# Two queues for one stream of weights: which engine issues the loads of the conditioning slots

## The chip, the cores and the metric

The kernel runs on one core of one Trainium2 chip. The metric is the device time in microseconds (us) of one execution, as the median of several runs. The engines are TensorE (PE in the profile, with its weight loads as PEld), VectorE (DVE), ScalarE (ACT), GpSimd (POOL) and SyncE (SP). SP does no arithmetic here: it issues the DMAs.

## The reference, cut to what matters

Two decoder layers over 256 tokens of width 2048, in float32. Each layer has a mixer (layer 0: sliding-window attention and a pooling mixer; layer 1: an mLSTM and block attention), then a gated feed-forward part with a short convolution. Every part is wrapped in RMSNorm and in a conditioning that is computed from one vector `c`:

```
c_act = silu(c)
mod = c_act @ ada_w[layer] + ada_b[layer]          # 2048 -> 6 x 2048
sh_m, sc_m, gt_m, sh_f, sc_f, gt_f = split(mod, 6)
h = rms_norm(x, norm_mix_pre) * (1 + sc_m) + sh_m
x = x + gt_m * rms_norm(mixer(h), norm_mix_post)
h = rms_norm(x, norm_ffn_pre) * (1 + sc_f) + sh_f
x = x + gt_f * rms_norm(conv_ffn(h), norm_ffn_post)
```

The twelve sections of `mod` need 2 x 2048 x 12288 weights, each used once, for a product of one vector with a matrix. All other weights are used for products with 256 tokens.

## The kernel before, in words

All weights stream from HBM once, in tiles of 1 MB (128 partitions x 2048 floats). Two kinds of tile share the pool `wst`, told apart by a tag:

- Tag "w", three slots: the weights of the products with 256 tokens ("split weights"). `load_split` (line 306) loads a tile and splits each half of it into a high and a low part, the high one by ACT (line 303), the low one by DVE (line 304), so that TensorE can multiply in three terms (`mm3`, lines 339 to 341) or two (`Halves.add`, lines 358 and 361). Six buffers hold high halves and five hold low halves.
- Tag "a", two slots (`SLOTS = (3, 2)`, line 25): the weights of the conditioning. They come in four streams. `ada_first` (line 523) multiplies 8 tiles on TensorE (line 532), `ada_gate` (line 541) another 16 (line 547), and `ada_rows` (line 558) handles the other 168: one DVE instruction multiplies a tile by the vector `c_row` and sums along it (line 564), and a short add of the bias follows (line 565). Of the 8 tiles of `ada_first` and of the 24 of `ada_m`, which `ada_rows` takes first, every other one goes into a "w" slot instead (`ATAG = "aw"`, line 27). So 4 + 12 + 16 + 144 = 176 loads go through the two "a" slots.

The conditioning is worked off behind the rest: `Behind.push` (line 257) emits the next tile's load and its arithmetic, and `Behind.step` (line 266), called once for each `load_split`, pushes at a pace that the kernel sets for each stage (up to 2 tiles for each tile of split weights in layer 0's mixer, between 0.2 and 1 in the feed-forward part). `need` pushes what is due before a norm.

Every load, of either tag, is issued by line 299 from SP, and SP issues in order. So a load of one kind that waits for its slot holds back those of the other kind behind it. A slot of tag "w" comes free when DVE has made the low part of the second half (line 304); a slot of tag "a" when line 564 has read it (or TensorE at line 547). POOL has 48 short instructions: constants at the start, masks (lines 238 to 242), and memsets of attention, pooling and gate tiles (lines 748, 860, 945, 969, 971). Each engine's order, POOL's and SP's among them, is laid down when the program is built.

In time the stages are: to about 38 us the start (x, the vector c, `ada_first`); to about 165 us layer 0's combined input projection (`first_of_all`) beside `ada_m`; to about 345 us attention, pooling and the output projection of layer 0 beside `ada_gate` and the first of the DVE rows; then layer 0's feed-forward part, layer 1's mixer from about 1100 us and its feed-forward part from about 1470 us. The DVE rows end near 1610 us.

Of the kernel before, what the change touches and what calls it, by code (L numbers as in the profile page):

```python
# [178 lines left out]
def trunk(ctx: ExitStack, tc: tile.TileContext, A, out):  # L179
    nc = tc.nc  # L180
# [115 lines left out]

    def load(src, shape=(128, NK, 128), tag="w"):
        w = wst.tile(list(shape), F32, name="w", tag=tag, bufs=SLOTS[tag == "a"])
        nc.sync.dma_start(w, src)
        return w  # L300

    def split(src, hi, lo):
# [3 lines left out]
    def load_split(src, shape=(128, NK, 128), later=False):  # L306

        w = load(src, shape)
        n = shape[1]
        parts = []  # L310

        def half(i):
            a, b = (n // 2) * i, n if i else n // 2
            hi = whp.tile([128, b - a, shape[2]], F32R, name="whi", tag="whi")
            lo = wlp.tile([128, b - a, shape[2]], F32R, name="wlo", tag="wlo")
            with ExitStack() as queue:
                if behind.splits > 0:
                    behind.splits -= 1
                    for ins in behind.marks:
                        queue.enter_context(tc.issue_after(ins))  # L320
                split(w[:, a:b, :], hi, lo)
            parts.append((hi, lo))
        half(0)
        if not later:
            half(1)
        behind.step()

        def at(i, m=1):
            if i < 0:
                return half(1)  # L330
            i, j = divmod(i, n // 2)
            if m == 1:
                return tuple(p[:, j, :] for p in parts[i])
            return tuple(p[:, j:j + m, :].rearrange("p a b -> p (a b)") for p in parts[i])
        return at
# [187 lines left out]
    def ada_first():  # L523

        for i, s in enumerate((SC_M, SH_M)):
            ps = bank((128, 4, 32))
            for k4 in range(4):
                w = load(A["ada_pe"][i, k4], (128, 4, 512), ATAG[k4 % 2])
                for r in range(4):
                    k = 4 * k4 + r  # L530
                    for j in range(4):
                        nc.tensor.matmul(ps[32 * j:32 * j + 32], c_rep[:, k, :], w[:, r, 128 * j:128 * j + 128],
                                         start=k == 0, stop=k == NK - 1, tile_position=(0, 32 * j))
                if k4 < 3:
                    yield
            tr = sml.tile([128, 4, 32], F32, name="tr", tag="t", bufs=4)
            nc.vector.transpose(tr.rearrange("p a b -> p (a b)"), ps.rearrange("p a b -> p (a b)"))
            nc.vector.tensor_tensor(mod[0, s][:, 0:4], tr[:, :, 0], ada_b(0, s)[:, 0:4], op=OP.add)
            yield

    def ada_gate():

        ps = bank((128, 512))
        for k in range(NK):
            w = load(A["ada_g"][k], (128, 1, D), "a")
            for j in range(4):
                nc.tensor.matmul(ps[32 * j:32 * j + 32, :], c_rep[:, k, :], w[:, 0, 512 * j:512 * j + 512],  # L547
                                 start=k == 0, stop=k == NK - 1, tile_position=(0, 32 * j))
            if k < NK - 1:
                yield  # L550
        for i in range(2):
            c = slice(8 * i, 8 * i + 8)
            tr = sml.tile([128, 8, 32], F32, name="tr", tag="t", bufs=4)
            nc.vector.transpose(tr.rearrange("p a b -> p (a b)"), ps[:, 256 * i:256 * i + 256])
            nc.vector.tensor_tensor(mod[0, GT_M][:, c], tr[:, :, 0], ada_b(0, GT_M)[:, c], op=OP.add)
        yield
# [646 lines left out]
```

## Time and profile before

| What | Value |
|---|---|
| median of 3 runs (lowest to highest) | 2221.96 us (2221.46 to 2225.73) |
| the profiled execution's own time | 2221.93 us |
| its span, first to last instruction | 2220.2 us |
| mean granted TensorE clock | 0.979 of full |
| busy: PE, DVE, ACT, POOL | 97%, 76%, 52%, 0% |
| moved by DMA | 578.42 MB, 261 GB/s on average |

The profiled execution lies 0.03 us below the median, and its time is 1.7 us longer than its span. A busy PE is not PE at its peak, since ends of matmuls are modelled; the granted clock of a stretch says at which of its two levels TensorE ran.

### The profile page before, as it was taken

The page shows a single profiled execution, that of the slowest core. Times are in us where ns is not written, and L with a number is a line of the kernel's source. Part 1 is how long each engine was busy: PE and PEld are TensorE (multiplying, and loading weights), DVE is VectorE, ACT ScalarE, POOL GpSimd, SP SyncE. Part 2 cuts the span into 40 slices and gives each one's busy share as a digit, 9 for nine tenths or more (in the row PEclk, how much of TensorE's full clock was granted, in tenths as well). Part 3 has the DMA queues.
Part 4 walks back from the last instruction along what each step waited for, and adds up shares of the span by engine and source line. Part 5 has one row for each costly group of instructions (what it writes and reads, how often), then busy time and mean ns, then how long its engine had stood idle before and what let it go on. Part 6 is the DMA issues. An engine that isn't in the chain of part 4 may idle for free.

```text
span 2220.2 us, 31418 instructions
## 1 busy us (share of the span) xinstructions
PE 2143.8 (97%) x12390; PEld 1857.7 (84%) x12390; DVE 1686.2 (76%) x2533; ACT 1153.6 (52%) x1790; POOL 10.4 (0%) x48
## 2 busy tenths in 40 slices
PE   7888998999999999999899999989999999999998
PEld 5886677997888888888797898878888888888886
DVE  4896798898899899887799867579955665665566
ACT  3345655464555455445576655555545544554453
POOL 1000000000000000000000000000000000000000
PEclk8899998999999999999999999989999999999999
DMA  9987886889889888887387635558855555555553
GB/s 372 348 334 280 322 339 258 328 310 350 308 325 341 331 322 332 330 332 263 135 300 275 229 132 190 190 189 307 319 209 184 188 197 189 190 188 194 188 190 114
DMA packets 81373, 578.42 MB, mean 261 GB/s; under 512 B 9156, under 2 KB 9156, under 8 KB 11464
## 3 DMA queue, kind: packets, MB, share of 16 engines
q1 hardware_dynamic: 81224, 576.40, 70.5%
q8 instruction: 97, 1.59, 0.3%
q14 instruction: 52, 0.43, 0.1%
HBM read 574.27 MB, written 2.10 MB: 260 GB/s over the span
## 4 chain that ended last, share of the span: by engine, by line
PE 90%; DVE 6%; ACT 2%; DMA 1%; issue 1%; SPq 0%; DVEq 0%; ACTq 0%
PE ps L358 28%; PE ps L361 15%; PE ps L340 14%; PE ps L339 14%; PE ps L341 14%; DVE w L564 2%; DVE wlo L304 2%; ACT g L582 1%; PE ps L758 1%; PE ps L547 1%; ACT whi L303 0%; PE ps L795 0%; PE ps L805 0%; DVE x L696 0%; DMA x<-in_x_dram 0%
## 5 line engine op out<-in xcount | busy, mean ns | idle before, releaser
L304 DVE TENSOR_TENSOR wlo<-w,whi 128x1024 fp32r<-128x1024 f32 (+1 forms) x706 | 847.7, 1218 | 314.9 <-PE ps L340 155.6
L303 ACT ACTIVATE whi<-w 128x1024 fp32r<-128x1024 f32 (+1 forms) x706 | 737.4, 1055 | 587.0 <-PE ps L341 281.4
L358 PE MATMUL ps<-g,whi 128*128 128x512 f32 x2736 | 654.4, 391 | 0.0
L358 PEld LDWEIGHTS ps<-g,whi 128*128 128x128 f32 x2736 | 501.9, 188 | 100.5 <-issue 1.2
L340 PE MATMUL ps<-wlo,g 128*128 128x512 f32 (+1 forms) x1152 | 429.1, 373 | 2.2 <-DVE wlo L304 2.2
L339 PE MATMUL ps<-whi,g 128*128 128x512 f32 (+1 forms) x1152 | 428.8, 373 | 0.3 <-ACT g L303 0.2
L341 PE MATMUL ps<-whi,g 128*128 128x512 f32 (+1 forms) x1152 | 428.2, 372 | 0.6 <-DVE g L304 0.6
L564 DVE SCALAR_TENSOR_TENSOR w<-w,c_row 128x2048 f32<-128x2048 f32 x168 | 383.7, 2285 | 3.9 <-DMA w<-in_ada_dve_dram 3.8
L361 PEld LDWEIGHTS ps<-g,wlo 128*128 128x128 f32 x2736 | 350.5, 191 | 13.6
L361 PE MATMUL ps<-g,wlo 128*128 128x256 f32 x2736 | 354.9, 283 | 0.0
L340 PEld LDWEIGHTS ps<-wlo,g 128*128 128x128 f32 x1152 | 217.1, 188 | 42.9 <-DVE wlo L304 4.0
L339 PEld LDWEIGHTS ps<-whi,g 128*128 128x128 f32 x1152 | 216.9, 188 | 40.5 <-issue 1.9
L341 PEld LDWEIGHTS ps<-whi,g 128*128 128x128 f32 x1152 | 216.9, 188 | 38.7 <-DVE g L304 1.5
L339 PE MATMUL ps<-g,whi 128*128 128x256 f32 x800 | 234.9, 297 | 13.7 <-ACT whi L303 7.1
L340 PE MATMUL ps<-g,whi 128*128 128x256 f32 x800 | 235.0, 295 | 0.3 <-DVE g L630 0.3
L341 PE MATMUL ps<-g,wlo 128*128 128x256 f32 x800 | 231.3, 294 | 1.4 <-DVE wlo L304 1.3
L339 PEld LDWEIGHTS ps<-g,whi 128*128 128x128 f32 x800 | 161.2, 203 | 17.3 <-ACT whi L303 8.7
L340 PEld LDWEIGHTS ps<-g,whi 128*128 128x128 f32 x800 | 161.8, 202 | 2.4 <-DVE g L630 2.3
L341 PEld LDWEIGHTS ps<-g,wlo 128*128 128x128 f32 x800 | 160.4, 202 | 2.4 <-DVE wlo L304 2.0
L366 ACT ACTIVATE low<-ps 128x256 f32<-128x256 f32 x156 | 59.5, 381 | 94.8 <-PE ps L361 94.4
L1133 DVE SCALAR_TENSOR_TENSOR z<-low,smalls,z 128x255 f32<-128x255 f32 (+1 forms) x148 | 71.3, 482 | 25.1 <-ACT z L1131 23.5
L1131 ACT ACTIVATE z<-low,smalls 128x256 f32<-128x256 f32 x74 | 44.6, 602 | 84.5 <-DVE low L367 84.5
(195 smaller groups left out, 1173.8 us busy)
## 6 DMA issues: line engine op xcount, KB each, us to landing
w<-in_up_dram SPq DMA_DIRECT2D x148, 1024.0 KB, 4.8
w<-in_ada_dve_dram SPq DMA_DIRECT2D x144, 1024.0 KB, 6.9
w<-in_down_dram SPq DMA_DIRECT2D x88, 1024.0 KB, 4.8
w<-in_up_first_dram SPq DMA_DIRECT2D x28, 1024.0 KB, 7.7
w<-in_ada_m_dram SPq DMA_DIRECT2D x24, 1024.0 KB, 7.5
w<-in_ev_first_dram SPq DMA_DIRECT2D x20, 1024.0 KB, 7.1
w<-in_ada_g_dram SPq DMA_DIRECT2D x16, 1024.0 KB, 4.8
w<-in_ev_out_dram SPq DMA_DIRECT2D x16, 1024.0 KB, 7.8
```

The lines of the kernel that those rows point to most:

```text
L303: nc.scalar.activation(hi, src, AF.Copy)
L304: nc.vector.tensor_tensor(lo, src, hi.bitcast(F32), op=OP.subtract)
L339: nc.tensor.matmul(ps, lh, rh, start=first, stop=False, **kw)
L340: nc.tensor.matmul(ps, lh, rl, start=False, stop=False, **kw)
L341: nc.tensor.matmul(ps, ll, rh, start=False, stop=last, **kw)
L358: nc.tensor.matmul(self.ps.rearrange("p a b -> p (a b)"), w(k)[0], act(k).both, start=k == 0, stop=False, skip_group_check=True)
L361: nc.tensor.matmul(self.ps[:, 0, :], w(k)[1], act(k)[0], start=False, stop=k == NK - 1, skip_group_check=True)
L366: nc.scalar.activation(low, self.ps[:, 1, :], AF.Copy)
L547: nc.tensor.matmul(ps[32 * j:32 * j + 32, :], c_rep[:, k, :], w[:, 0, 512 * j:512 * j + 512], start=k == 0, stop=k == NK - 1, tile_positio ...
L564: nc.vector.scalar_tensor_tensor(w, w, 1.0, c_row, op0=OP.mult, op1=OP.mult, accum_out=m)
L1131: nc.scalar.activation(z, pg, AF.Identity, scale=cw(2, f), bias=sm(f"ffn_b{l}", f))
L1133: nc.vector.scalar_tensor_tensor(z[:, lag:], pg[:, :T - lag], cw(2 - lag, f), z[:, lag:], op0=OP.mult, op1=OP.add)
```

## The change

The issuing engine of a load is now chosen by its tag: loads into the two "a" slots are issued from GpSimd's queue, all others from SyncE's as before. Slots, order of the calls, sizes and arithmetic are the same.

```
     def load(src, shape=(128, NK, 128), tag="w"):
         w = wst.tile(list(shape), F32, name="w", tag=tag, bufs=SLOTS[tag == "a"])
-        nc.sync.dma_start(w, src)
+        (nc.gpsimd if tag == "a" else nc.sync).dma_start(w, src)
         return w
```

## Rows read from the trace of the kernel before

**Rows 1.** The page: busy times by engine, and the chain that ended last.

```profile
PE 2143.8 (97%) x12390; PEld 1857.7 (84%) x12390; DVE 1686.2 (76%) x2533; ACT 1153.6 (52%) x1790; POOL 10.4 (0%) x48
...
PE 90%; DVE 6%; ACT 2%; DMA 1%; issue 1%; SPq 0%; DVEq 0%; ACTq 0%
```

**Rows 2.** Stretches: us, PE PEld DVE ACT POOL busy, PE clock, DMA share, GB/s.

```profile
38.00:165.00 127.00, 114.19 (x815) 110.17 (x816) 112.83 (x150) 49.03 (x61) 0.00 (x0) 0.89 0.91 346
165.00:250.00 85.00, 78.89 (x495) 52.84 (x496) 51.17 (x151) 45.74 (x113) 0.67 (x6) 0.96 0.78 283
250.00:345.00 95.00, 87.03 (x408) 67.72 (x404) 88.94 (x160) 55.85 (x127) 1.90 (x4) 0.99 0.87 336
...
500.00:1050.00 550.00, 548.91 (x2890) 472.50 (x2889) 476.52 (x633) 279.32 (x369) 0.00 (x0) 1.00 0.86 324
```

**Rows 3.** Waits of SP's queue, whole span: us in total, times, longest.

```profile
SPq L299 <- DVE wlo L304: 1426.0, 305, 11.0
SPq L299 <- DVE mod L565: 157.0, 38, 9.9
SPq L299 <- DVE w L564: 133.2, 42, 6.7
...
SPq L299 <- PE ps L547: 36.5, 15, 5.9
```

**Rows 4.** Timelines of SP and PE at the start: start us, us, instruction.

```profile
1.24 1.37 SPq L299 DMA_DIRECT2D w<-in_ada_pe_dram  x3
...
17.91 7.19 PE L896 MATMUL ps<-g,ones 1*128 1x512 f32 x8 [4.85 <-DMA g<-in_c_row_dram]
```

**Rows 5.** Waits of PE (40 to 165 us) and DVE (80 to 160 us); one stretch, columns of rows 2.

```profile
PE ps L339 <- ACT whi L303: 3.4, 5, 1.6
...
DVE g L434 <- PE ps L341: 5.6, 6, 1.1
...
101.30:104.70 3.40, 3.40 (x18) 3.40 (x18) 2.64 (x3) 2.00 (x2) 0.00 (x0) 0.50 0.99 398
```

**Rows 6.** Timelines of SP and PE, and PE's waits, 186 to 250 us.

```profile
189.61 17.43 SPq L299 DMA_DIRECT2D w<-in_ada_g_dram  x6
...
194.43 1.94 PE L547 MATMUL ps<-w,c_rep 128*32 128x512 f32 x8 [0.55 <-DMA w<-in_ada_g_dram]
...
205.59 1.06 PE L547 MATMUL ps<-w,c_rep 128*32 128x512 f32 x8 [0.87 <-DMA w<-in_ada_g_dram]
...
PE ps L878 <- DVE pdiff L871: 4.7, 4, 2.2
```

**Rows 7.** Timeline of POOL: start us, us, instruction [idle before, releaser].

```profile
3.86 0.42 POOL L248 TENSOR_SCALAR_AFFINE_SELECT after<-after 128x256 f32<-128x256 f32 x1
...
278.62 1.06 POOL L239 TENSOR_SCALAR_AFFINE_SELECT dist<-dist 128x256 f32<-128x256 f32 x1
...
1127.17 0.52 POOL L969 MEMSET g<- 128x512 f32 x1 [18.42 <-PE ps L624]
```

**Rows 8.** Timelines of SP and DVE, landing of in_ada_dve, PE's waits; 250 to 345 us.

```profile
254.02 4.34 SPq L299 DMA_DIRECT2D w<-in_ada_dve_dram  x2
...
251.70 2.29 DVE L564 SCALAR_TENSOR_TENSOR w<-w,c_row 128x2048 f32<-128x2048 f32 x1
...
261.13 2.29 DVE L564 SCALAR_TENSOR_TENSOR w<-w,c_row 128x2048 f32<-128x2048 f32 x1
...
309.18 2.29 DVE L564 SCALAR_TENSOR_TENSOR w<-w,c_row 128x2048 f32<-128x2048 f32 x1 [0.36 <-DMA w<-in_ada_dve_dram]
...
DMA to landing us min/median/max: 4.7/6.3/6.4
...
PE ps L340 <- DVE wlo L304: 2.0, 3, 1.2
```

**Rows 9.** Timeline of DVE: two instructions on 256 elements.

```profile
35.49 0.29 DVE L629 CAST g<-h 128x256 fp32r<-128x256 f32 x1 [0.69 <-ACT h L627]
35.82 0.42 DVE L630 TENSOR_TENSOR g<-h,g 128x256 fp32r<-128x256 f32 x1
```

More of the change, by code (lines that the diff above doesn't have):

```diff
@@ L298, in load @@
         w = wst.tile(list(shape), F32, name="w", tag=tag, bufs=SLOTS[tag == "a"])
-        nc.sync.dma_start(w, src)
+        (nc.gpsimd if tag == "a" else nc.sync).dma_start(w, src)
         return w
```

## The prediction

> **What bounds the kernel now.** I read the page first. TensorE is busy for 97% of the span and the chain that ended last lies on it for 90%, on DVE for 6% and on DMA for 1% [rows 1]. So the loads as such are hardly on the path: a change of queues can win or lose only where TensorE waits, or where DVE or ACT, which feed it, wait. The table by stretch says where that can be. From 500 to 1050 us TensorE is busy for 548.91 of 550 us at full clock, though 0.86 of the DMA time is taken: nothing can be won there, and a late conditioning load is covered by TensorE's own work. The three earlier stretches are different: 38 to 165 us (DVE busy for 112.83 of 127, DMA 0.91, clock 0.89), 165 to 250 us, and 250 to 345 us (DVE 88.94 of 95) [rows 2]. There three engines and the DMAs run close together, and any one may give or take a few microseconds.
>
> The waits of SP's own queue show what the change is about. SP stands 1426.0 us waiting for the split of a weight tile, which is the normal state of a queue that prefetches into three slots. But it also stands 157.0 + 133.2 + 36.5 = 326.7 us because an "a" slot is still being read by lines 564/565 or 547 [rows 3]. For that time a load of split weights behind it could not start. Now the two are separated.
>
> **The change part by part.** The profiled execution took 2221.93 us, span 2220.2, and the sum is made against that; it is 0.03 us below the median of the runs shown. A measurement of this kernel can tell about 0.2%, or 4.4 us, from no change.
>
> 176 issues leave SP's queue, and 176 arrive in POOL's. No byte, slot or instruction on another engine is added or removed. SP's saved issue time (1.37 us for three, under 0.5 us each [rows 4]) is worth nothing by itself: SP waits far longer than it issues.
>
> **What POOL needs for an issue** is not in this trace. From below it costs nothing over SP. From above it costs POOL's costliest instruction, 1.06 us [rows 7], plus a whole 2.29 us DVE instruction [rows 8] if the two hinder each other: 3.35 us. I take 1.06 us, since an instruction of POOL is the nearest row, and call it the delay. By the Trainium skill (DMA: Bandwidth & Descriptors, section "Latency and other measured facts") the first byte comes about 0.4 us later on the GpSimd path than on the SP path; with that for the delay, terms 3 and 4 below would shrink to about 0.7 us together and the sum to about +0.7 us. No row here shows it.
>
> *Term 1, the start.* SP issues the first three tiles of `ada_first` at 1.24 us [rows 4]. Two of them move to POOL, which stands in its constants until 4.28 us (3.86 + 0.42) [rows 7]. TensorE waits 4.85 us at 17.91 for the pieces of `c_row`, which lie behind these tiles and x on SP's queue [rows 4]. If the moved tiles let x and `c_row` through first, up to 4.85 us is won; if TensorE must instead take them later, ahead of line 896, about as much as they are late (4.28 - 1.24 + 1.06 = 4.1 us) is lost. The bytes ahead of `c_row` stay about the same and share the same transfers. I take 0.
>
> *Term 2, 38 to 165 us.* Loads of split weights no longer wait behind `ada_m`. TensorE loses 3.4 us there to late high halves, and after such a gap the clock fell to 0.50 for 3.4 us [rows 5], which costs half of that, 1.7 us. But DVE's order is fixed and it is nearly full: in 80 to 160 us it is idle for long only for TensorE, 5.6 us in 6 waits [rows 5]. So the gain is between 0 and 5.6 us; since DMA is 0.91 busy and has little room to deliver earlier, I take 1.5 us.
>
> *Term 3, `ada_gate`, 186 to 250 us.* Here TensorE itself reads the "a" slots. The load issued at 189.61 is used at 194.43, 4.82 us later, and TensorE has waited 0.55 us for it; another wait of 0.87 us ends at 205.59 [rows 6]. A load cannot be issued earlier than now, as its slot comes free when TensorE has read it. So each of these two is late by the whole delay, 2 x 1.06 = 2.1 us, less what TensorE would spend waiting for the pooling tiles anyway (4.7 us in 4 waits [rows 6]). Bounds 0 and 2 x 3.35 = 6.7 us; I take 1.5 us.
>
> *Term 4, the DVE rows, 250 to 316 us.* The slot that DVE frees at 253.99 (251.70 + 2.29) gets its load at 254.02 and is read at 261.13: 7.1 us for a landing that takes 4.7 to 6.4 us, median 6.3. Nine of the twelve loads from here to the one used at 309.18 have between 6.3 and 7.4 us, 6.9 on average, and that last one already makes DVE wait 0.36 us [rows 8]. With 1.06 us added the median landing is 7.4 us, 0.5 us over: 9 x 0.5 = 4.5 us. The two slots alternate and DVE is one engine, so a delay for one slot gives the other the same room: half, some 2 us. TensorE passes it on, since by 320 us its lead over line 304 is used up (2.0 us of waits [rows 8]). Bounds: 0, and with 3.35 us 9 x (6.3 + 3.35 - 6.9) / 2 = 12.4 us. The split-weight loads go out earlier in this stretch, but no wait of TensorE here is for one. I take 2 us.
>
> *Term 5, POOL's own order.* POOL's 48 instructions [rows 1] now share a queue with loads that wait for slots. A memset at line 969 stands 18.42 us for TensorE [rows 7]; a load behind it would stand as long. Only prefetches can be caught so: a load whose reader stands ahead of what the memset waits for must stand ahead of the memset, or nothing would move. That is two loads at most, one for each slot. The other way round, the six short instructions of POOL between 165 and 250 us (0.67 us [rows 2]) feed the pooling tiles and can be held by a load that waits for `ada_gate`. From 0 to 18.42 us; I take 1.5 us, about one delay for each of the two.
>
> From 500 us on I take nothing: the cover is TensorE's 548.91 of 550 us. Were it gone, DVE's waits for these loads would show in TensorE's.
>
> Sum: 0 - 1.5 + 1.5 + 2 + 1.5 = +3.5 us, **2225.4 us**, 0.16% above before: no change that could be told.
>
> **The rivals.**
>
> *Slower: the delay is near its upper bound.* Place: the slot cycles of terms 3 and 4, which have no room (waits of 0.55, 0.87 and 0.36 us already stand there). It decides from a delay of about 1.5 us. At 3.35 us: 6.7 + 12.4 + 1.5 = 20.6 us, about 2242 us. For it: the "a" slots are only two deep and each load goes out at the instant its slot is free. Against it: nothing in the trace shows a GpSimd issue being slow. The Trainium skill (SBUF — State Buffer, "The 'DVE blocks DMA' trap (SWDGE)") says that a GpSimd issue cannot write its descriptors while DVE runs a two-port instruction. What such a rule would do here is read from two rows: the CAST of 256 elements takes 0.29 us where a TENSOR_TENSOR of as many takes 0.42 [rows 9], so the fast kind is short here, and lines 304 and 564, which fill DVE, are not of it; the block would be about 0.3 us, and only if it held for line 564 too would the time be that of this rival. Half of my chance for slower comes from a smaller delay (1.5 to 2 us), which ends near 2230.
>
> *Faster: separation pays in full.* No delay, so terms 3 to 5 vanish, and term 2 reaches its bound: 2221.93 - 5.6 = 2216.3 us; with half of term 1's gain, 2214. For it: 326.7 us of SP's waits for "a" slots. Against it: the chain has no load on it after the start.
>
> *The change does little of what it says.* 16 conditioning loads of tag "w" stay on SP, all of them before 165 us. Then term 2 is 0 and the time is 2227; it is part of "same" and "slower".
>
> **How the numbers follow.** No change: 0.40 (2217.5 to 2226.4 is its own range). Slower: 0.38, of which two thirds with a delay of 1.5 us or more and the rest from POOL's order. Faster: 0.22, as terms 1 and 2 can only together beat 4.4 us. The range from 2214 to 2246 takes in the faster case and the slow one with a few half-clock stretches of 1.7 us each on top; it leaves out some 0.08 above and 0.08 below.
>
> **What would show it.** Right: TensorE's waits for `in_ada_g` grow from 1.4 us (0.55 + 0.87) by some 1 to 2 us; DVE's waits for `in_ada_dve` between 250 and 316 us grow from 0.36 to a few us; landings of in_ada_dve there rise by about 1 us; SP's waits on lines 564, 565 and 547 shrink to those of the tag "w" tiles; 500 to 1050 us stays as it is. Wrong: a landing longer by 3 us or more, or DVE's own instructions lengthened (the slow rival); waits for high halves before 165 us gone and the clock there above 0.89 (the fast one); a long wait of POOL with a load right behind it (term 5 mis-sized).

## The result, and the profile after

The kernel before takes 2221.7 us on this chip, the changed one **2284.1 us** (2282.7 to 2286.3). The ratio is 1.0283, with a 95% interval of 1.0265 to 1.0302: 62 us slower, far outside the forecast's range. The profiled execution has a span of 2281.0 us (before 2220.2).

The page of the changed kernel, read as [rows 1] were: busy times, the two queues of loads, the chain that ended last, the groups of line 564 and of GpSimd's issues, and the landings.

```profile
PE 2154.1 (94%) x12390; PEld 1865.0 (82%) x12390; DVE 1686.8 (74%) x2533; ACT 1145.3 (50%) x1790; POOL 104.4 (5%) x224
...
q1 hardware_dynamic: 55880, 391.84, 46.5%
q0 software_dynamic: 25344, 184.56, 22.0%
...
PE 68%; DVE 12%; DMA 11%; issue 7%; ACT 2%; POOL 0%; SPq 0%; DVEq 0%; POOLq 0%; ACTq 0%
...
L564 DVE SCALAR_TENSOR_TENSOR w<-w,c_row 128x2048 f32<-128x2048 f32 x168 | 383.6, 2287 | 52.7 <-DMA w<-in_ada_dve_dram 46.3
...
L299 POOL DMA_DIRECT2D w<-in_ada_dve_dram x144 | 76.1, 528 | 1318.9 <-DVE w L564 1173.4
...
w<-in_up_dram SPq DMA_DIRECT2D x148, 1024.0 KB, 4.9
w<-in_ada_dve_dram POOLq DMA_DIRECT2D x144, 1024.0 KB, 5.3
```

TensorE's share of the chain falls from 90% to 68%; DMA goes from 1% to 11% and DVE from 6% to 12%. DVE now stands 46.3 us for in_ada_dve at line 564. Before, that wait was 3.8 us:

```profile
L564 DVE SCALAR_TENSOR_TENSOR w<-w,c_row 128x2048 f32<-128x2048 f32 x168 | 383.7, 2285 | 3.9 <-DMA w<-in_ada_dve_dram 3.8
```

So the loads of the conditioning have come onto the path. They did not become slow: their median landing is 5.3 us (before 6.9), and an issue takes POOL 0.53 us.

Next, the stretches, with the columns of [rows 2], the first one before and then both after:

```profile
345.00:500.00 155.00, 148.40 (x1183) 145.48 (x1184) 137.05 (x205) 81.86 (x123) 0.00 (x0) 0.96 0.79 301
```

```profile
345.00:500.00 155.00, 132.15 (x990) 128.93 (x989) 132.23 (x194) 73.69 (x113) 12.67 (x24) 0.89 0.80 307
500.00:1050.00 550.00, 528.64 (x2784) 454.62 (x2783) 450.78 (x605) 251.58 (x346) 34.84 (x66) 0.99 0.81 305
```

From 345 to 500 us TensorE is busy for 132.15 us where it was 148.40, at a clock of 0.89 instead of 0.96. From 500 to 1050 us it is no longer full: 528.64 of 550 us, where [rows 2] have 548.91. The same points of the program, in us from the start of the span, tell how the loss adds up (line 618 begins a norm's product, line 358 is the down projection):

```
point of the program                before    after   behind by
first line 618 instruction            28.6     32.4     3.8
line 618, before layer 0's ffn       346.5    351.7     5.2
first line 358 instruction             569      591      22
the 769th of line 358                  967     1020      53
line 618, layer 1's mixer           1105.3   1158.6    53.3
line 618, layer 1's ffn             1463.0   1525.4    62.4
```

Up to 346 us the loss is 5.2 us, near the forecast's +3.5. The other 57 us come where the forecast has nothing: 17 between 346 and 569 us, 31 more by 967 us, and the last 9 in layer 1's mixer (1105 to 1463 us).

**What is different there** is the rate of the conditioning. Line 564 by stretch, first before, then after (us, DVE busy for line 564 with two records for each row, PE clock, DMA share, GB/s):

```profile
500.00:750.00 250.00, 73.90 (x67) 1.00 0.88 331
750.00:900.00 150.00, 46.89 (x41) 1.00 0.88 329
900.00:1105.00 205.00, 35.62 (x32) 1.00 0.72 267
```

```profile
500.00:750.00 250.00, 95.28 (x84) 0.99 0.91 348
750.00:900.00 150.00, 55.10 (x48) 0.98 0.90 342
900.00:1105.00 205.00, 0.00 (x0) 1.00 0.56 195
```

The changed kernel works off 66 rows from 500 to 900 us instead of 54, then none at all. The DMAs are 0.90 busy or more while the rows run, and about half idle afterwards. The issues of 500 to 900 us, before and after (KB of each, median us to landing), show what was displaced:

```profile
w<-in_ada_dve_dram SPq DMA_DIRECT2D x53, 1024.0 KB, 7.6
w<-in_up_dram SPq DMA_DIRECT2D x48, 1024.0 KB, 4.9
w<-in_down_dram SPq DMA_DIRECT2D x25, 1024.0 KB, 5.0
```

```profile
w<-in_ada_dve_dram POOLq DMA_DIRECT2D x66, 1024.0 KB, 5.9
w<-in_up_dram SPq DMA_DIRECT2D x41, 1024.0 KB, 6.8
w<-in_down_dram SPq DMA_DIRECT2D x24, 1024.0 KB, 6.6
```

There are 13 more conditioning tiles and 8 fewer tiles of split weights, and each split-weight tile lands 1.6 to 1.9 us later.

The rows did not merely arrive earlier: they **stand earlier in DVE's queue**. Each engine's order is laid down when the program is built, and the one-line change altered that order, though it touches no instruction of DVE. The table counts the splits (line 304) that stand on DVE ahead of the n-th row (line 564). A tile of split weights has two splits. The last column is the time from the 73rd row to the 121st, divided by the tiles between them.

```
kernel                     n=61   n=73   n=85   n=97  n=121  n=133   us per tile
before                      118    153    185    220    285    346      5.51
after                       105    134    151    177    221    345      6.32
```

The 121st row stands 64 splits, or 32 tiles, further forward. In that stretch the changed kernel asks for 48 rows in 43.5 tiles, 2.10 loads per tile; before, it was 48 in 66, 1.73 loads. At 1.049 MB a load and TensorE's pace of 5.51 us, that would need 2.10 x 1.049 / 5.51 = 0.400 MB per us, 400 GB/s. What these stretches show, before and after, with the columns of [rows 2]:

```profile
582.47:946.10 363.63, 363.63 (x1949) 315.36 (x1948) 323.53 (x436) 185.13 (x248) 0.00 (x0) 1.00 0.88 330
```

```profile
553.75:828.85 275.10, 258.49 (x1310) 218.95 (x1308) 241.01 (x316) 114.22 (x156) 25.35 (x48) 0.99 0.93 355
```

The DMAs moved 355 GB/s, at which rate a tile takes 2.10 x 1.049 / 0.355 = 6.21 us; 6.32 was measured. That checks the count, but it does not prove that the DMAs are the limit, since rate and time are of the same stretch. DVE has too much to do as well: its busy time for a tile was 323.53 / 66 = 4.90 us and is now 241.01 / 43.5 = 5.54 us, just over TensorE's 5.51. No run here separates the two.

One such step on the timeline of DVE in the changed kernel (start us, us, instruction, [idle before, releaser]), then of POOL's queue and of TensorE:

```profile
589.12 2.29 DVE L564 SCALAR_TENSOR_TENSOR w<-w,c_row 128x2048 f32<-128x2048 f32 x1
...
596.03 1.22 DVE L304 TENSOR_TENSOR wlo<-w,whi 128x1024 fp32r<-128x1024 f32 x1
601.32 2.29 DVE L564 SCALAR_TENSOR_TENSOR w<-w,c_row 128x2048 f32<-128x2048 f32 x1 [4.07 <-DMA w<-in_ada_dve_dram]
...
608.71 2.36 DVE L304 TENSOR_TENSOR wlo<-w,whi 128x1024 fp32r<-128x1024 f32 x2
```

```profile
591.71 0.53 POOL L299 DMA_DIRECT2D w<-in_ada_dve_dram  x1 [4.03 <-DVE w L564]
```

```profile
610.00 2.08 PE L361 MATMUL ps<-g,wlo 128*128 128x256 f32 x8 [3.10 <-DVE wlo L304]
```

DVE frees the slot at 591.41 (589.12 + 2.29). The load goes out at once and is used at 601.32, 9.6 us later. DVE stands 4.07 us for it, while the next splits stand behind in its queue, and TensorE waits 3.10 us for the one that begins at 608.71. The waits of 560 to 960 us (DVE, then PE) show the hand-over; before, TensorE has no wait in this stretch:

```profile
DVE w L564 <- DMA w<-in_ada_dve_dram: 30.1, 15, 4.9
...
PE ps L361 <- DVE wlo L304: 12.1, 7, 4.6
PE ps L340 <- DVE wlo L304: 9.3, 5, 3.0
```

### The profile page after: what moved, and what is told of

Its sections match the earlier page's. It is cut to its first block, busy times and chain, and to the rows that moved or that the text cites. A ratio compares the mean times of both kernels' runs of the same rounds, so it can differ in the third digit from the quotient of the medians.

```text
span 2281.0 us, 31562 instructions
## 1 busy us (share of the span) xinstructions
PE 2154.1 (94%) x12390; PEld 1865.0 (82%) x12390; DVE 1686.8 (74%) x2533; ACT 1145.3 (50%) x1790; POOL 104.4 (5%) x224
## 3 DMA queue, kind: packets, MB, share of 16 engines
q0 software_dynamic: 25344, 184.56, 22.0%
## 4 chain that ended last, share of the span: by engine, by line
PE 68%; DVE 12%; DMA 11%; issue 7%; ACT 2%; POOL 0%; SPq 0%; DVEq 0%; POOLq 0%; ACTq 0%
PE ps L358 22%; PE ps L361 11%; PE ps L339 11%; PE ps L340 10%; PE ps L341 10%; DMA w<-in_ada_dve_dram 5%; DVE w L564 5%; DVE wlo L304 4%; DMA w<-in_ada_g_dram 1%; DMA w<-in_ev_first_dram 1%; ACT g L582 1%; DMA w<-in_up_dram 1%; DMA w<-in_ada_m_dram 1%; ACT whi L303 1%; DMA g<-in_c_row_dram 0%
## 5 line engine op out<-in xcount | busy, mean ns | idle before, releaser
L564 DVE SCALAR_TENSOR_TENSOR w<-w,c_row 128x2048 f32<-128x2048 f32 x168 | 383.6, 2287 | 52.7 <-DMA w<-in_ada_dve_dram 46.3
L361 PE MATMUL ps<-g,wlo 128*128 128x256 f32 x2736 | 358.5, 284 | 12.1 <-DVE wlo L304 12.1
L299 POOL DMA_DIRECT2D w<-in_ada_dve_dram x144 | 76.1, 528 | 1318.9 <-DVE w L564 1173.4
```

The source lines that it names most:

```text
L299: (nc.gpsimd if tag == "a" else nc.sync).dma_start(w, src)
L361: nc.tensor.matmul(self.ps[:, 0, :], w(k)[1], act(k)[0], start=False, stop=k == NK - 1, skip_group_check=True)
L564: nc.vector.scalar_tensor_tensor(w, w, 1.0, c_row, op0=OP.mult, op1=OP.mult, accum_out=m)
```

## The experiments

Two theories stood at first. **Order**: with the separate queue the rows run ahead of their places, and their rate fills the DMAs. **Path**: GpSimd's queue is itself a dear path for loads. For each kernel the ratio to the kernel before is given with its 95% interval.

**1. All loads from GpSimd.**

```
-        nc.sync.dma_start(w, src)
+        nc.gpsimd.dma_start(w, src)
```

> All 546 weight loads, of both tags, are issued from GpSimd's queue, in one order as before; the built order of DVE is nearly that of before (the 121st row of line 564 behind 284 instructions of line 304; 285 before, 221 after the change). Order theory (the loss comes from DVE rows and their loads running ahead of their places once their queue is free of the split weights' queue): 2215 to 2235 us, PE busy for over 545 of 550 us between 500 and 1050 us. Path theory (a transfer issued from GpSimd is itself slower to start or to land, or takes more of the DMA engines): at least as slow as after the change, 2280 us or more, since three times as many loads take that path.

Measured: 2237.6 us, ratio 1.0077 (1.0058 to 1.0095). The rows stand among the splits as before (121st row behind 284 splits, 5.48 us per tile), though other instructions of DVE and TensorE changed places, and the stretch that had failed is nearly full:

```profile
500.00:1050.00 550.00, 546.64 (x2908) 473.19 (x2907) 480.52 (x638) 279.69 (x370) 88.68 (x170) 1.00 0.86 327
```

All 546 loads take the supposedly dear path, and only 16 us are lost, against 62. The path theory cannot explain the result. The profiled execution is 11 us longer than the one before, and 10 of them are lost by the line 618 instruction before layer 0's feed-forward part (356.5 us against 346.5).

**2. The change, with the rows tied to the splits.** The row is held, in the order that is laid down, behind the latest split. Lines move by 4.

```
 def push(self):
+    if self.last is not None:
+        after_norm.enter_context(tc.issue_after(self.last))
...
+    behind.last = split(w[:, a:b, :], hi, lo).ins
```

> The change, with one thing added: what a push emits on DVE stands behind the last split (line 304) emitted before it, so rows of line 564 can no longer be laid ahead of their places (the 121st row behind 302 instructions of line 304). Queues as after the change. Order theory: the loss between 345 and 1105 us is gone, 2215 to 2232 us. Path theory, or one in which two queues that share the DMA engines delay the split weights: 2265 us or more, as the queues are the same.

Measured: 2234.6 us, ratio 1.0058 (1.0039 to 1.0076). The queues are those of the change; the 121st row stands behind 302 splits. 49.5 of the 62 us are gone, and TensorE is busy for 549.45 of 550 us from 500 to 1050 us. Layer 1's mixer takes 358.1 us again (before 357.7, changed kernel 366.8), so its 9 us belong to the order too; by which wait was not followed. Some 13 us remain.

**3 and 4. One half of the loads each**: only the 144 of in_ada_dve, then only the 32 of in_ada_pe, in_ada_m and in_ada_g.

```
+        (nc.gpsimd if tag == "a" and late else nc.sync).dma_start(w, src)
...
+        (nc.gpsimd if tag == "a" and early else nc.sync).dma_start(w, src)
```

> Only the 144 loads of ada_dve are issued from GpSimd; ada_pe, ada_m and ada_gate are back on SP. The built order of DVE from the 49th row on is that of after the change. Order theory: nearly the whole loss, 2272 to 2286 us (62 less the 4 to 6 us that the first 345 us lost). If the loss came from the start or from ada_gate's slot cycle: under 2245 us.

> The other half: ada_pe, ada_m and ada_gate's 32 loads are issued from GpSimd, the 144 of ada_dve from SP. DVE's built order from the 49th row on is that of before. Order theory: 2222 to 2232 us, the 4 to 6 us that the first 345 us lost and no more. Otherwise over 2245 us.

Measured: in_ada_dve alone 2278.1 us, ratio 1.0256 (1.0231 to 1.0282), with the order of the changed kernel. The 32 early loads alone: 2226.4 us, ratio 1.0026 (1.0015 to 1.0036), with the order of before from the 49th row on. Nearly all of the loss belongs to the 144 loads, about 5 us to the others.

**5 and 6. Order without the second queue.** All loads stay on SP. Kernel 5 has the tie of experiment 2 and nothing else. Kernel 6 changes one constant, so that 1.1 rows are laid for each weight tile in the feed-forward part of layer 0, in place of 0.65.

```
-ADA_PACE = (0.65, 0.35, 0.2)
+ADA_PACE = (1.1, 0.35, 0.2)
```

> The kernel before, all weight loads on SyncE's queue, with the tie of the paced kernel alone: each conditioning row is laid behind the latest split, so row 121 of DVE stands behind 302 splits, in before behind 285. If the tie costs nothing by itself, the 13 us that the paced kernel kept are those of GpSimd's queue, most of them in the first 345 us, and this kernel takes 2216 to 2226 us. If the tie is what costs (rows laid late, with TensorE waiting for their result), it takes 2228 to 2236 us, and the early stage (first line 618 instruction at 346 us) is as before.

> All weight loads on SyncE's queue, as before; one constant makes the program lay 1.1 conditioning rows for each weight tile in place of 0.65, so row 121 stands behind 228 splits (before 285, changed kernel 221). Theory of the order (rows that come faster than one per weight tile fill the DMAs and make split weights late, whatever the queue): 2260 to 2290 us, TensorE busy for 535 us or less of 500 to 1050 us. Rival, the theory of the two queues (the loss needs conditioning loads that overtake split weights on a queue of their own; on one queue, in order, they cannot): 2218 to 2235 us.

Measured: the tie costs nothing by itself, 2222.3 us, ratio 1.0009 (0.9998 to 1.0020). So the 13 us that experiment 2 kept come with GpSimd's queue. The fast rows cost even more than the change does, with no load on GpSimd (they run on to 1105 us, where the changed kernel has none after 900): **2292.7 us, ratio 1.0323 (1.0304 to 1.0343)**. That kernel's stretch, and its issues of 500 to 900 us:

```profile
500.00:1050.00 550.00, 503.34 (x2523) 422.19 (x2522) 498.46 (x654) 227.76 (x312) 0.00 (x0) 0.98 0.89 348
```

```profile
w<-in_ada_dve_dram SPq DMA_DIRECT2D x70, 1024.0 KB, 6.8
w<-in_up_dram SPq DMA_DIRECT2D x42, 1024.0 KB, 9.2
```

It has 48 rows in 44 tiles and takes 6.29 us for a tile: nearly the figure of the changed kernel, on one queue. What differs is who waits. On one queue DVE stands only 2.2 us for in_ada_dve from 500 to 1050 us, and the split weights are late instead: TensorE waits 29.0 us for high halves of line 303 and 14.8 us for low halves of line 304.

**7. The change turned round**: conditioning from SP, split weights from GpSimd.

```
+        (nc.sync if tag == "a" else nc.gpsimd).dma_start(w, src)
```

> The change turned round: conditioning loads stay on SyncE's queue, the split weights go out from GpSimd's. The order of DVE is that of the changed kernel (row 121 behind 221 splits). Theory of the order: as slow as the changed kernel, 2270 to 2300 us, with TensorE's gaps at the same place. Rival, GpSimd's path is what makes the conditioning loads costly: 2220 to 2250 us, since they are off it, and TensorE's stretch from 500 to 1050 us nearly full.

Measured: 2285.8 us, ratio 1.0293 (1.0268 to 1.0318), with the rows where the changed kernel has them (121st row behind 221 splits) and 6.22 us per tile. For the loss it does not matter which of the two kinds goes out from GpSimd, only that they are on different queues.

```
kernel                        n=61  n=85  n=121  us per tile      time
before                         118   185    285     5.51        2221.7
all from GpSimd (1)            118   185    284     5.48        2237.6
tie, all on SP (5)             118   192    302     5.53        2222.3
after                          105   151    221     6.32        2284.1
swapped (7)                    105   151    221     6.22        2285.8
1.1 rows a tile, on SP (6)     118   162    228     6.29        2292.7
```

**8 and 9. What a separate queue costs when the order is right.** Only in_ada_dve from GpSimd, with the tie: in kernel 8 to the split nine before the latest, in kernel 9 to the latest.

```
+                if len(self.laid) > self.lag:
+                    after_norm.enter_context(tc.issue_after(self.laid[-1 - self.lag]))
```

> Only the 144 in_ada_dve loads go out from GpSimd's queue, and each row is laid behind the split that is nine before the latest, so row 121 stands behind 295 splits (before 285, the same edit without the tie 221 and 2278 us). Theory of the order: nearly the whole loss is gone, 2216 to 2228 us, and TensorE is busy for over 546 us of 500 to 1050 us. Rival, the two queues cost by themselves while they share the DMAs: 2250 us or more.

> Only the 144 in_ada_dve loads from GpSimd's queue, and each row laid behind the latest split: DVE's order is that of the kernel with the tie alone on SyncE's queue (2222.3 us), row 60 behind 118 splits. Theory of sharing: what the separate queue still costs when the order is right is that split weights no longer stand behind a conditioning load and so run beside it; the rows' landings in 345 to 500 us rise from a median of 6.0 to about 7.2 us, DVE waits some 11 us for them in 250 to 500 us (0 with one queue), TensorE's busy time in 345 to 500 us is about 142 us (148), and the time is 2228 to 2234 us. Rival, the 2239.7 us of the looser tie came from its order alone (row 60 behind 110): 2219 to 2225 us.

Measured: kernel 8 takes 2239.7 us, ratio 1.0084 (1.0060 to 1.0107), between the two expectations. It holds TensorE at 549.95 of 550 us from 500 to 1050 us, but its 61st row is behind 110 splits rather than 118, and it arrives at the first line 358 instruction at 592 us (kernel 9: 576; kernel 8's profiled execution is the longest of its six).

Kernel 9: 2228.4 us, ratio 1.0033 (1.0020 to 1.0045), 6 us over kernel 5. The two have the same order of DVE up to 250 us and nearly the same from 500 us on, but not in between: there some rows of kernel 9 stand up to two splits earlier, and TensorE's order moved as well. So, other than the expectation says, the queue is not the only difference. The longest wait of DVE in 250 to 500 us and the issues of 345 to 500 us, in kernel 5, where none of DVE's waits of over 1 us is for a row:

```profile
DVE g L633 <- ACT h L631: 9.3, 6, 6.0
```

```profile
w<-in_up_first_dram SPq DMA_DIRECT2D x21, 1024.0 KB, 8.3
w<-in_ada_dve_dram SPq DMA_DIRECT2D x21, 1024.0 KB, 5.9
```

and in kernel 9:

```profile
DVE w L568 <- DMA w<-in_ada_dve_dram: 11.6, 8, 2.8
```

```profile
w<-in_up_first_dram SPq DMA_DIRECT2D x21, 1024.0 KB, 6.9
w<-in_ada_dve_dram POOLq DMA_DIRECT2D x21, 1024.0 KB, 7.0
```

The two kinds of load exchange their delays: the split weights land 1.4 us sooner, the rows 1.1 us later. I read it so: on one queue a split-weight load stands behind a conditioning load that waits for its slot, so that load has the DMAs more to itself; on two queues it shares them. The queue that stood for the conditioning slots would then have been a priority. One thing supports this reading: 10.8 of the 11.6 us are waits for rows that stand within one DVE instruction of their place in kernel 5. What the moved order of TensorE costs there was not tested.

**10. Kernel 9 with the sides changed**: conditioning on SP, split weights from GpSimd once the in_ada_dve rows have begun.

```
+        behind.rows += late
+        (nc.gpsimd if tag == "w" and behind.rows else nc.sync).dma_start(w, src)
```

> As the run beside it, but the sides changed: conditioning loads on SyncE's queue, split weights from GpSimd's once the in_ada_dve rows have begun; the same order on DVE. Theory of sharing: it does not matter which of the two queues a load uses, 2228 to 2240 us, with DVE waiting 8 us or more for in_ada_dve in 250 to 500 us. Rival, it is GpSimd's own path (an issue 0.27 us later after its slot is free, its own landing): the rows are spared it, DVE's waits for them stay under 3 us and the time is 2219 to 2227 us.

Measured: 2233.7 us, ratio 1.0055 (1.0041 to 1.0069), as the theory of sharing has it; its order is nearly kernel 9's. DVE's wait for in_ada_dve in 250 to 500 us is 5.5 us, between the two expectations, and the landing in 345 to 500 us is 7.2 us, though these loads are on SP. The profiled execution (span 2225.1 us) was the shortest of the six, so its waits may understate. Sharing is supported, not shown; how much of kernel 9's 11.6 us belongs to GpSimd's later issue, or to the moved order, is not settled.

**11. Only the 16 in_ada_g loads.**

```
+            w = load(A["ada_g"][k], (128, 1, D), "a", True)
```

> Only the 16 in_ada_g loads from GpSimd's queue; the rest, and the order, as before. My prediction's term 3 says +1.5 us (0 to 6.7), TensorE's waits for in_ada_g up from 1.4 us to about 3. Together with the loads of in_ada_pe and in_ada_m the loss was 4.8 us; if the gate makes half of it or more, this takes 2224 to 2228 us, else (the start and the stretch to 165 us carry it) 2220 to 2223 us.

Measured: 2225.8 us, ratio 1.0025 (1.0013 to 1.0038): the loss of kernel 4 comes with these 16 loads. Against the expectation the order is not wholly that of before: between 150 and 350 us some instructions of DVE and TensorE changed places. TensorE's waits for them in 165 to 250 us:

```profile
PE ps L547 <- DMA w<-in_ada_g_dram: 6.2, 4, 2.2
```

In [rows 6] two waits of 0.55 and 0.87 us stand in its place, 1.4 us.

**12. The tie, with GpSimd from the 39th in_ada_dve load on**, about 500 us.

```
+        (nc.gpsimd if late and behind.rows > 38 else nc.sync).dma_start(w, src)
```

> The tie of the tight kernel, and only the in_ada_dve loads after the 38th (from about 500 us on) from GpSimd's queue. If the cover from 500 us on holds as long as the order is kept, as my prediction said without its condition, this is the time of the tie on SyncE's queue: 2219 to 2225 us, TensorE busy for over 548 us of 500 to 1050 us. If the second queue costs there as well, 2228 us or more.

Measured: 2221.2 us, ratio 1.0001 (0.9991 to 1.0012), TensorE 549.06 of 550 us. This is the cleanest pair: against kernel 5 TensorE's order is the same, and on DVE and ACT five instructions changed places. With the order kept, a second queue costs nothing where TensorE is full. None of the kernels beats the one before.

**The ledger** adds up: the order 2.2% (changed kernel less kernel 2), in_ada_dve on its own queue 0.33% (kernel 9), the gate 0.25% (kernel 11), the start and in_ada_m nothing that can be told (kernel 4 less kernel 11); together 2.8%. The second and third items hold what the queue costs and what the smaller moves of the order cost, unseparated.

## Why the prediction was wrong

**The step that failed** is "From 500 us on I take nothing: the cover is TensorE's 548.91 of 550 us". The cover is real as long as the order is kept (experiment 12). In the changed kernel it was gone, and it showed as the prediction said that it would, in TensorE's waits: 12.1 + 9.3 = 21.4 us for low halves between 560 and 960 us. For 345 to 500 us there was no term at all, and no reason for that; 17 us were lost between 346 and 569 us. There too the order decides: the four kernels whose 61st row stands behind 105 to 110 splits (changed kernel, 3, 7 and 8) have TensorE busy for 128.6 to 133.6 us of 345 to 500 us, those with 118 for 141.75 or more.

Beneath both lies one step. The prediction took DVE's order as given: term 2 says that it "is fixed", and term 5 treats POOL's order as the only new one. It asked how late each load would be at its place and never whether the places stay. They moved by up to 68 splits (the 130th row). The loss of some 50 us is not among the rivals either: the slow one was a delay, and this is loads that are asked for too soon.

A second reading led there. The 326.7 us of SP's waits [rows 3] were taken as harm to the split weights. They were none where TensorE is full: from 500 to 1050 us SP stood 71.7 us at lines 564 and 565 before (64.3 + 7.4), in kernel 12 not at all, and the time is the same. And not all were waits for conditioning slots: the changed kernel has no "a" load on SP, and yet one of the three rows stays.

```profile
SPq L299 <- DVE wlo L304: 1793.5, 320, 26.8
SPq L299 <- DVE mod L565: 162.0, 28, 23.0
...
SPq L299 <- DVE w L564: 18.7, 9, 2.7
```

The row names the last DVE instruction that SP's wait saw done, which may merely follow the split.

**The terms**, each by its own run:

- *The delay.* After a slot is free SP issues within 0.03 us [rows 8], POOL 0.30 us later (591.41 to 591.71). In 165 to 250 us the gate's median landing goes from 4.8 to 5.7 us in kernel 11 (over the whole run 4.8 and 6.5). Together that is 1.2 to 2.0 us, where 1.06 was taken. The Trainium skill (DMA: Bandwidth & Descriptors, section "Latency and other measured facts") puts the first byte about 0.4 us later on the GpSimd path. The gate's fastest landings in that stretch, 4.7 and 5.0 us, and the 0.27 us of later issue make 0.6, near that; what lies above it is, I think, the sharing of the DMAs, which no run shows alone.
- *Terms 1 and 2* (0 and -1.5 us): the start did lose 3.8 us, within its bounds, since TensorE waits 12.40 us for its first conditioning tile. In kernel 4, which loses 4.5 us there, the first pooling product (line 878) begins at 185.2 us (before 185.4): the loss is regained. In the changed kernel's profiled execution it begins at 188.5, still 3.1 us behind. So its 5.2 us at 346 us are 3.1 from these terms and 2.1 from the next three, where the forecast had -1.5 and +5: that the sums are near each other is luck.
- *Term 3* (+1.5, up to 6.7): in kernel 11 4.8 us more waiting and 4.7 us more time. That fits the mechanism told; it was sized from the two loads that were already late, but four were late in the end.
- *Term 4* (+2, up to 12.4): in kernel 9, DVE's waits of 250 to 345 us are 6.1 us and the line 618 instruction comes 4.3 us later, about twice the term. But the waits did not come from longer landings, as told: the median of 250 to 345 us is 5.4 us there and 6.3 before, and single loads were late (7.2 and 7.9 us before the two longest waits). Such waits went on to 500 us, where no term looked.
- *Term 5* (+1.5): not seen. In 165 to 250 us TensorE's wait for the pooling tiles went down, from 4.7 us [rows 6] to 3.1, with one new wait of 1.2 us beside it.
- *The slow rival*: a delay of 3.35 us did not happen; the 18 issues of 250 to 345 us took POOL 0.53 to 0.55 us each, though DVE was busy for 88.24 of the 95 us. Its smaller form (1.5 to 2 us, near 2230) is about what is left when the order is pinned: kernel 2, 2234.6 us. Its time was nearer than the forecast's, and still it does not hold the cause of the loss.

Of the signs looked for, the waits came: the gate's went from 1.4 to 6.0 us (some 1 to 2 more were told), line 564's between 250 and 316 us from 0.36 to 2.1. They were those of the 5 us, not of the 62. Three did not: the landing of in_ada_dve there fell instead of rising by about 1 us (median 6.3 us before, 5.3 after, of those that the traces have), SP's waits put down to line 565 did not shrink (157.0 and 162.0 us), and 500 to 1050 us did not stay as it was.

**What is argued, not shown**, is why the order moved. From the 49th row on the rows moved ahead whenever, without the tie, the in_ada_dve rows and the split weights were loaded from different queues (changed kernel, kernels 3 and 7), and not when these two shared one (kernels 1, 4 and 11). So the program that lays the order out seems to place a row when it believes its load to be ready; on one queue it reckons with the loads ahead. No run varied that belief.

## What to carry to other kernels

Before a shared in-order queue is split, ask what it keeps from starting too soon, in the order that is laid down as much as on the chip. After a change of queues, compare the order of every engine, instruction by instruction, before comparing waits, and if the order moved, pin it (experiment 2) to see which part of the result is the queue's. Count the loads per tile against what the DMAs move in that stretch: here 1.73 loads of 1 MB per 5.5 us fit, and 2.1 did not. Count the work of the engine that takes them, too: DVE's went from 4.90 to 5.54 us per tile.

## What was not expected of the hardware

- Loads issued by GpSimd appear under a queue of their own kind, q0 software_dynamic, and 25344 packets of it took 22.0% of the 16 engines' span, no more per byte than on q1: 0.119% per MB against 0.119%. Their issue costs 0.53 us of POOL where SP needs 0.33.
- The Trainium skill (DMA: Bandwidth & Descriptors, section "Issuing engines are not separate DMA queues") says that all issuing engines share the same 16 DMA engines, and that issuing from several saves only the time of the issue. The first half agrees: 5.9 and 8.3 us of landing on one queue became 7.0 and 6.9 on two. The second is not all that happened here: with rows and split weights on different queues, kernels 9 and 10 became 0.33% and 0.55% longer, not shorter, though part of that may be the moved order; in kernel 12, where the order was kept, nothing changed.
- With rows running ahead the DMAs moved 346 GB/s from 500 to 900 us, on two queues (changed kernel) as on one (kernel 6); before, 330. It is not the most that they can do: kernel 7 moved 366 GB/s from 38 to 165 us, and one slice of the changed kernel's page has 390. Whether this rate or DVE's work is why 6.2 to 6.3 us per tile comes out in three different kernels is not shown.
